# Seven half-size products for the up projections of the second FFN of a latent-diffusion backbone

## The chip, the cores and the metric

One Trainium2 chip; the program runs on one of its cores. Times are device microseconds of one execution, the median of the runs named beside them. The engines are TensorE (PE: matmuls; PEld: its weight loads), VectorE (DVE), ScalarE (ACT), GpSimd (POOL) and SyncE (SP, which issues most transfers). A granted TensorE clock of 1.00 is 2.4 GHz, one of 0.50 is 1.2 GHz.

## The reference

Two layers over 512 latent tokens and 256 context tokens of width 1024. Layer 0 mixes by attention, layer 1 by a bidirectional mLSTM; each is followed by a normalised, modulated, gated convolutional FFN with 2816 hidden channels. After layer 1 only the latent tokens are needed. What this document is about is the FFN of layer 1 and the normalisation ahead of it:

```python
x = x + gt2 * conv_ffn(modulate(rmsnorm(x, norm2_g[layer]), sh2, sc2),
                       ffn_w_up[layer], ffn_conv_w[layer], ffn_conv_b[layer], ffn_w_down[layer])

def conv_ffn(h, w_up, conv_w, conv_b, w_down):
    gate, val = jnp.split(jnp.dot(h, w_up), 2, axis=-1)
    return jnp.dot(jax.nn.silu(dwconv(gate, conv_w, conv_b)) * val, w_down)
```

`dwconv` is a convolution of width 3 over the tokens, channel by channel. Everything is float32.

## The kernel before

Activations lie with channels on the 128 partitions: `X` is [128, 8, 512], eight blocks of 128 channels by 512 tokens. To keep float32 accuracy a float32 product is made of three matmuls in the format float32r: both factors are cut into a high part (a cast, on ScalarE, L42) and a low part (the rest, a subtraction on VectorE, L43; together `split`), and high x high, low x high and high x low are added up in PSUM. `fm` (L77 to L86, its matmul is L85) does this for all blocks of the contraction.

Weights come in pieces of 512 KB. `weights` (L59) takes a raw tile `wr` of 128 x 1024, issues the load on SP (L66), and splits it into `wh` and `wl`. `wtile` (L48) hands these tiles out in turn: two buffers for `wr` at this point of the kernel, three each for `wh` and `wl`. A load waits until its raw buffer has been split, a split until the matmuls of its old contents are done.

PSUM has eight banks of 512 float32 columns: `A()` (L109) gives a pair of banks out of two pairs, `B(tags)` (L112) the banks T, U, R, O in turn, each one tile.

The hidden channels are 22 chunks of 128 (`NF`). `up(f)` (L319) makes one chunk: 24 matmuls of 512 columns for the gate, 24 for the value; the convolution (`conv`, L305 on ScalarE, L307 and L308 on VectorE), Silu (L339), the product with the value (L341), and the split of the result into `ah`, `al`. In chunks 0 to 3 of this layer `halves` cuts each matmul of 512 columns in two of 256, so that the first 256 tokens can be worked on while the second 256 are still being normalised. `down(fs)` (L359) takes a group of four chunks (the last group has two): for each of the eight output blocks 12 matmuls of 512 columns (L354) into one of the banks T, U, and an update of `X` on VectorE (`xupd`, L401). `ffn` runs up(0) to up(4), down of group 0, four more chunks, the next group, and so on; the last two groups come after all chunks. The last group's blocks are stored as soon as they are updated (L369).

Ahead of it (in `build`, at L1430) the last part of the layer's output projection runs in two halves of 256 tokens, six matmuls for each output block, and each half is followed by its norm: `norm_steps` (L256) sums squares (L269, L272 on ScalarE; L273 on VectorE and GpSimd), takes the reciprocal root, spreads it with a transpose into PSUM (L284), and then for each block of channels scales (`u`, L288, VectorE), adds the shift into the high part (L290, ScalarE), and forms the low part (L296 on VectorE for even blocks; L293 and L294 on ScalarE and GpSimd for odd ones).

The order of instructions on each engine is chosen by the framework when the program is built: it takes what it holds to be ready, by the order of the program text as priority. Each engine then runs its list strictly in order and waits where a semaphore says so. Tiles have their waits made by the framework.

Of the kernel before, what the change touches and what calls it, by code (L numbers as in the profile page):

```python
# [21 lines left out]
KD = 8  # L22
NF = 22
# [9 lines left out]
class Kernel:  # L33
    def __init__(self, tc, ins, out):
        self.tc, self.nc, self.i, self.out = tc, tc.nc, ins, out
        self.turn = {}


    def split(self, hi, lo, src, scale=None):
# [8 lines left out]
    def wtile(self, tag, n, cols, dt):  # L48

        bufs = [(self.wp, tag + "0"), (self.wp, tag + "1"), (self.wx, tag + "x")]  # L50
        if tag == "wr":
            del bufs[1]
        if self.wx is None:
# [202 lines left out]
    def norm_steps(self, pool, X, l, which, hh, hl, ranges):  # L256
# [4 lines left out]
        for t0, t1, c in ranges:  # L261
# [35 lines left out]

            steps += [lambda k=k, f=apply: f(k) for k in range(KD)]
        return steps


    def conv(self, y, ps, w, b, segs):
# [986 lines left out]
    def build(self):  # L1289
        tc, nc, i = self.tc, self.nc, self.i  # L1290
        with ExitStack() as es:
# [126 lines left out]
            gh = hp.tile([128, KD, NL], F32R, name="hh")  # L1418
            gl = hp.tile([128, KD, NL], F32R, name="hl")
            with tc.tile_pool(name="o1", bufs=1, reuse_waits="tile") as OP, \  # L1420
                    tc.tile_pool(name="nrm", bufs=1, reuse_waits="tile", side="right") as NP:
                x = [post(h, OP, "RO") for h in (6, 7)]
                for half in range(2):
                    t = slice(256 * half, 256 * half + 256)
                    for o in range(KD):
                        ps = self.B("TU")
                        m = 0
                        for (wh, wl), (xh, xl) in zip(ws, x):
                            for a, b in ((wh, xh), (wl, xh), (wh, xl)):
                                nc.tensor.matmul(ps[:, 0:256], a[:, o * 128:(o + 1) * 128], b[:, t],  # L1430
                                                 start=m == 0, stop=m == 5)
                                m += 1
                        self.xupd(1, 16, X, ps, o, 256 * half, 256, 0)
                    self.norm(NP, X, 1, 1, gh, gl, [(256 * half, 256 * half + 256, 0)])
            RP.release()


            with tc.tile_pool(name="ffn1", bufs=1, reuse_waits="tile") as FP:
                self.ffn(1, X, gh, gl, FP, NL, [])
            hp.release()  # L1440
            HP.release()

# [103 lines left out]
```

## Time and profile before

| what | value |
|---|---|
| median of 3 runs | 1748.17 us (1747.02 to 1748.54) |
| the profiled execution's own time | 1747.95 us |
| its span, first to last instruction | 1746.1 us |
| granted TensorE clock, mean | 0.989 |
| matmuls | 9622 |
| TensorE, VectorE, ScalarE, GpSimd busy | 96%, 72%, 43%, 15% of the span |
| moved by DMA | 169.43 MB, 97 GB/s on the mean |

Busy time of TensorE counts a matmul from its start to its modelled end, and matmuls overlap, so a busy TensorE is not one at its peak; how long a matmul takes in a stream is read from the distance of their starts, or from a block of the chain of waits divided by its count. The chain of waits follows the work that ended last backwards from the last instruction, at each step to what released it. "Idle" in a group of instructions is the time its engine stood still just before them.

### The profile page before, as it was taken

What the parts mean: (1) busy time and instruction counts of PE and PEld (TensorE: products, weight loads), DVE (VectorE), ACT (ScalarE), POOL (GpSimd) and SP (SyncE); (2) the same over time, 40 slices, a digit from 0 to 9 for tenths busy, and PEclk for the clock granted to TensorE, in tenths of its full rate; (3) what the DMA queues carried; (4) which work ended last, traced back from release to release, by engine and by line L of the source; (5) the groups of instructions that cost most, each with busy time, mean ns of one, the idle gap of its engine ahead of it and who ended that gap; (6) DMA issues with size and microseconds to landing.
All of it is one profiled execution on the core that took longest, in us unless ns stands there. A gap on an engine that the chain in (4) does not pass through costs nothing.

```text
span 1746.1 us, 25308 instructions
## 1 busy us (share of the span) xinstructions
PE 1673.7 (96%) x9622; PEld 1439.8 (82%) x9622; DVE 1250.8 (72%) x2310; ACT 749.6 (43%) x1394; POOL 261.3 (15%) x304
## 2 busy tenths in 40 slices
PE   6998898999999999999999989999999999999999
PEld 2787787888878888888888878888788898888887
DVE  7998889987787586675758467768778854444444
ACT  4336788986252132221312246645553542232231
POOL 0342545552120000000000023112110200000000
PEclk9999999999999999999999999999998999999999
DMA  8450000005344343342424233111112133323332
GB/s 315 127 167 24 11 11 13 14 1 207 107 140 150 97 146 120 124 154 88 154 85 134 72 121 98 61 50 37 61 43 103 61 109 97 97 97 97 98 97 96
DMA packets 73442, 169.43 MB, mean 97 GB/s; under 512 B 8292, under 2 KB 36964, under 8 KB 72936
## 3 DMA queue, kind: packets, MB, share of 16 engines
q1 hardware_dynamic: 73316, 167.80, 29.5%
q8 instruction: 76, 1.25, 0.3%
q14 instruction: 46, 0.38, 0.1%
q10 hardware_dynamic: 4, 0.01, 0.0%
HBM read 163.59 MB, written 4.20 MB: 96 GB/s over the span
## 4 chain that ended last, share of the span: by engine, by line
PE 73%; DVE 14%; ACT 7%; issue 3%; POOL 1%; DMA 1%; DVEq 0%; ACTq 0%; POOLq 0%; SPq 0%
PE psS L85 31%; PE psT L354 7%; PE psU L354 6%; PE psU L85 4%; PE psR L85 3%; PE psT L85 2%; DVE junk L138 2%; PE S L447 2%; PE psO L492 2%; PE psR L354 1%; PE psO L354 1%; ACT p L455 1%; PE state L1213 1%; DVE wl L43 1%; PE psT L95 1%
## 5 line engine op out<-in xcount | busy, mean ns | idle before, releaser
L85 PE MATMUL psS<-hl,wh 128*128 128x512 f32 (+1 forms) x992 | 346.8, 351 | 2.6 <-POOL hl L294 2.6
L85 PE MATMUL psS<-hh,wh 128*128 128x512 f32 (+1 forms) x992 | 347.0, 350 | 0.4 <-ACT hh L290 0.4
L85 PE MATMUL psS<-hh,wl 128*128 128x512 f32 (+1 forms) x992 | 346.1, 350 | 0.0
L42 ACT CAST wh<-wr 128x1024 fp32r<-128x1024 f32 (+2 forms) x187 | 193.4, 1036 | 338.6 <-PE psO L354 113.0
L43 DVE TENSOR_TENSOR wl<-wr,wh 128x1024 fp32r<-128x1024 f32 (+2 forms) x187 | 227.6, 1218 | 47.3 <-ACT wh L42 47.0
L85 PEld LDWEIGHTS psS<-hl,wh 128*128 128x128 f32 x992 | 186.8, 189 | 29.4 <-POOL hl L294 4.1
L85 PEld LDWEIGHTS psS<-hh,wh 128*128 128x128 f32 x992 | 186.8, 188 | 26.6 <-ACT hh L290 1.1
L85 PEld LDWEIGHTS psS<-hh,wl 128*128 128x128 f32 x992 | 186.6, 188 | 25.6
L307 DVE SCALAR_TENSOR_TENSOR y<-psS,fcw,y 128x511 f32<-128x511 f32 (+1 forms) x60 | 39.5, 658 | 143.3 <-ACT y L305 143.3
L138 DVE CUSTOM_DVE_ANT_0 y<-ar,cb 128x1024 f32<-128x1024 f32 x112 | 136.5, 1219 | 0.3 <-DMA ar<-in_ada 0.3
L305 ACT ACTIVATE y<-psS,fcb,fcw 128x512 f32<-128x512 f32 (+1 forms) x60 | 40.3, 705 | 205.3 <-PE psS L85 205.3
L273 POOL TENSOR_TENSOR sa<-sa,sq 128x256 f32<-128x256 f32 (+1 forms) x18 | 17.9, 993 | 637.1 <-ACT sq L272 637.1
L401 DVE SCALAR_TENSOR_TENSOR X<-psU,mod,X 128x512 f32<-128x512 f32 (+1 forms) x69 | 48.0, 696 | 87.3 <-PE psU L354 77.0
L458 POOL TENSOR_SCALAR p<-p,rs 128x768 f32<-128x768 f32 (+1 forms) x96 | 73.9, 776 | 114.7 <-DVE rs L457 70.5
L138 DVE CUSTOM_DVE_ANT_0 junk<-ar,cb 128x1024 f32<-128x1024 f32 x64 | 81.8, 1278 | 0.4
L341 DVE TENSOR_TENSOR y<-y,psS 128x512 f32<-128x512 f32 (+1 forms) x60 | 34.1, 597 | 52.8 <-PE psS L85 52.8
L354 PE MATMUL psT<-ah,wh 128*128 128x512 f32 x176 | 68.8, 391 | 1.8 <-DVE X L401 1.8
L339 ACT ACTIVATE y<-y 128x768 f32<-128x768 f32 (+1 forms) x44 | 32.6, 740 | 84.7 <-DVE y L308 84.7
L354 PE MATMUL psU<-ah,wh 128*128 128x512 f32 x176 | 68.7, 390 | 0.0
L354 PE MATMUL psU<-ah,wl 128*128 128x512 f32 x176 | 68.7, 390 | 0.0
L354 PE MATMUL psT<-ah,wl 128*128 128x512 f32 x176 | 68.7, 390 | 0.0
L354 PE MATMUL psU<-al,wh 128*128 128x512 f32 x176 | 68.5, 389 | 0.0
(674 smaller groups left out, 4382.9 us busy)
## 6 DMA issues: line engine op xcount, KB each, us to landing
ar<-in_ada SPq DMA_DIRECT2D x88, 512.0 KB, 3.5
wr<-in_wup SPq DMA_DIRECT2D x88, 512.0 KB, 3.4
wr<-in_wdn SPq DMA_DIRECT2D x44, 512.0 KB, 3.3
pr<-in_adak SPq DMA_DIRECT2D x8, 512.0 KB, 5.3
wr<-in_w_out SPq DMA_DIRECT2D x8, 512.0 KB, 3.5
wr<-in_w_mqk SPq DMA_DIRECT2D x8, 512.0 KB, 3.5
wr<-in_w_mv SPq DMA_DIRECT2D x8, 512.0 KB, 4.0
wr<-in_w_mo SPq DMA_DIRECT2D x8, 512.0 KB, 3.4
```

The costliest lines, as they stand in the source:

```text
L42: nc.scalar.copy(hi, src)
L43: nc.vector.tensor_tensor(lo, src, f32(hi), op=SUB)
L85: nc.tensor.matmul(ps, a, b[:, k, x0:x0 + n], start=i == 0, stop=i == 3 * nk - 1)
L138: nc.vector.tensor_tensor_reduce(out, raw, self.cb[:, c], 1.0, 0.0, MUL, ADD, self.mraw[l][:, n, c:c + 1])
L305: nc.scalar.activation(y[:, t0:t0 + n], p, AF.Identity, bias=b, scale=w[1])
L307: nc.vector.scalar_tensor_tensor(y[:, t0 + 1:t0 + n], p[:, 0:n - 1], w[0], y[:, t0 + 1:t0 + n], op0=MUL, op1=ADD)
L341: nc.vector.tensor_tensor(y[:, t0:t0 + n], y[:, t0:t0 + n], p, op=MUL)
L354: nc.tensor.matmul(ps[:, 0:n], x[:, off:off + 128], y[:, t0:t0 + n], start=m == 0, stop=m == 3 * len(fs) - 1)
L401: self.nc.vector.scalar_tensor_tensor(X[:, o, t0:t0 + n], ps[:, 0:n], self.mod[l][:, g0 + o, c:c + 1], X[:, o, t0:t0 + n], op0=MUL, op1=ADD)
L447: nc.tensor.matmul(s[:, c0:c0 + n], q[:, q0:q0 + 128], k[:, k0 + c0:k0 + c0 + n], start=m == 0, stop=m == len(passes) - 1)
L458: nc.gpsimd.tensor_scalar(p[:, 0:nk], p[:, 0:nk], r, 1.0, op0=MUL, op1=MUL)
L492: nc.tensor.matmul(out, a, b, start=st, stop=sp)
```

## The change

It replaces `norm` and `ffn` of layer 1 by `norm_seven` and `ffn_seven`; layer 0 keeps the old ones.

The up projection of a chunk is seen as a product of 2 x 2 blocks: the contraction in two halves of four channel blocks, the tokens in two halves of 256, and gate and value as the two rows. Seven products of half blocks (12 matmuls of 256 columns each) replace the eight (96 of 256, or 48 of 512). The sums of token halves that they need (T1 to T4) are made once, in `norm_seven`; the sums of weight blocks for each chunk: `R[:, 0]` and `R[:, 2]` are the value's second half and the gate's first half, each plus the value's first half, `R[:, 1]` is `R[:, 0]` plus the gate's first half. They are made by loading one summand three times over on SP and adding the others with two transfers that accumulate, issued by GpSimd; `R[:, 3]` adds the gate's second half to `R[:, 1]` on VectorE. Four pieces are split a chunk: the gate (A1), R0 and R1 (S12), R2 and R3 (S34), and the value's second half (`d`, half as long).

The products of a chunk share two accumulators: Y, one bank of a pair that two chunks share, and W, the second half of the bank whose first half is Z. Y is read after product 1, after 6, after 7 and after 4 while it goes on accumulating, W after product 5 and after 3. The loop is written out so that the products of chunk f stand between those of chunk f-1, with a step of the down projection (one output block, 12 matmuls of 512 columns) at two places of each turn. `wtile` gets one more buffer for each of the three tags.

```diff
+    def norm_seven(self, pool, X, l, B, half, n, kept):
...
+        for k in range(KD):
+            u = pool.tile([128, n], F32, tag="u", name="u", bufs=3)
+            nc.vector.scalar_tensor_tensor(u, X[:, k, t0:t1], s[:, k, 0:1], rb[:, 0:n], op0=MUL, op1=MUL)
+            sh = self.mod[l][:, 24 + k, 0:1]
+            nc.scalar.activation(h[:, k], u, AF.Identity, bias=sh)
+            if half == 0:
+                nm, kk = ("B11", k) if k < 4 else ("B21", k - 4)
+                nc.scalar.activation(B[nm][0][:, kk], u, AF.Identity, bias=sh)
+                low(nm, kk, h[:, k], nc.gpsimd if k % 2 else nc.vector)
+        if half == 0:
+            return
+        g = kept[0]
+        k2 = [(slice(a, a + 2), slice(a + 4, a + 6)) for a in (0, 2)]
+
+        for a, b in k2:
+            nc.vector.tensor_tensor(g[:, a], g[:, a], h[:, a], op=SUB)
+            nc.scalar.copy(B["T1"][0][:, a], g[:, a])
+            low("T1", a, g[:, a], nc.vector)
+        for a, b in k2:
+            nc.scalar.copy(B["B22"][0][:, a], h[:, b])
+            low("B22", a, h[:, b], nc.gpsimd)
+            nc.vector.tensor_tensor(h[:, a], h[:, b], h[:, a], op=SUB)
+            nc.vector.tensor_tensor(h[:, b], h[:, b], g[:, a], op=ADD)
+            nc.scalar.mul(B["T2"][0][:, a], h[:, b], -1.0)
+            nc.vector.scalar_tensor_tensor(B["T2"][1][:, a], h[:, b], -1.0, f32(B["T2"][0][:, a]), op0=MUL, op1=SUB)
+        for a, b in k2:
+            nc.scalar.copy(B["T3"][0][:, a], h[:, a])
+            low("T3", a, h[:, a], nc.gpsimd)
+        for a, b in k2:
+            nc.vector.tensor_tensor(g[:, b], h[:, b], g[:, b], op=SUB)
+            nc.scalar.copy(B["T4"][0][:, a], g[:, b])
+            low("T4", a, g[:, b], nc.vector)
+
+    def ffn_seven(self, l, X, B, pool):
...
+        def prod(ps, w, x, first, last):
+            m = 0
+            for k in range(4):
+                for a, b in ((w[0], x[0]), (w[1], x[0]), (w[0], x[1])):
+                    nc.tensor.matmul(ps, a[:, k], b[:, k], start=first and m == 0, stop=last and m == 11,
+                                     skip_group_check=True)
+                    m += 1
...
+        def load(f):
+            c = ch[f] = {}
+            g, v = i["wup"][l, f, 0], i["wup"][l, f, 1]
+            c["a"] = self.wtile("wr", KD, 128, F32)
+            nc.sync.dma_start(c["a"], g)
+            R = c["R"] = pool.tile([128, 4, 4, 128], F32, tag="R", name="R", bufs=2)
+            for j, src in enumerate((v[:, 4:8], v[:, 4:8], g[:, 0:4])):
+                nc.sync.dma_start(R[:, j], src)
+            c["d"] = pool.tile([128, 4, 128], F32, tag="d", name="d", bufs=2)
+            nc.sync.dma_start(c["d"], v[:, 4:8])
+            nc.gpsimd.dma_start(R[:, 0:3], v[:, 0:4].unsqueeze(1).to_broadcast([128, 3, 4, 128]), accum_op=ADD)
+            nc.gpsimd.dma_start(R[:, 1], g[:, 0:4], accum_op=ADD)
+
+        def p1(f):
...
+            c["A1"] = pair(c["a"])
+            prod(c["Y"], part(c["A1"], 0), B["B11"], True, False)
+
+        def p2(f):
+            c = ch[f]
+            zw = self.B("TU")
+            c["W"], Z = zw[:, n:2 * n], zw[:, 0:n]
+            prod(Z, part(c["A1"], 1), B["B21"], True, True)
+            g = c["g"] = pool.tile([128, nt], F32, tag="g", name="g", bufs=2)
+            nc.scalar.copy(g[:, 0:n], Z)
+            nc.vector.tensor_tensor(g[:, 0:n], g[:, 0:n], c["Y"], op=ADD)
+
+        def p5(f):
+            c = ch[f]
+            c["S12"] = pair(c["R"][:, 0:2].rearrange("p s k c -> p (s k) c"))
+            prod(c["W"], part(c["S12"], 0), B["T1"], True, False)
+            p = c["p5"] = pool.tile([128, n], F32, tag="p5", name="p5", bufs=2)
+            nc.scalar.copy(p, c["W"])
+
+        def p6(f):
+            c = ch[f]
+            prod(c["Y"], part(c["S12"], 1), B["T2"], False, False)
+            u = c["u2"] = pool.tile([128, n], F32, tag="u2", name="u2", bufs=2)
+            nc.scalar.copy(u, c["Y"])
+
+        def p3(f):
+            c = ch[f]
+            R = c["R"]
+            nc.vector.tensor_tensor(R[:, 3], R[:, 1], c["a"][:, 4:8], op=ADD)
+            c["S34"] = pair(R[:, 2:4].rearrange("p s k c -> p (s k) c"))
+            prod(c["W"], part(c["S34"], 1), B["B22"], False, True)
+            g = c["g"]
+            nc.vector.tensor_tensor(g[:, n:nt], c["u2"], c["W"], op=ADD)
...
+        def p7(f):
+            c = ch[f]
+            prod(c["Y"], part(c["S34"], 0), B["T3"], False, False)
+            v = c["v2"] = pool.tile([128, n], F32, tag="v2", name="v2", bufs=2)
+            nc.vector.tensor_tensor(v, c["p5"], c["Y"], op=ADD)
+
+        def p4(f):
+            c = ch[f]
+            prod(c["Y"], pair(c["d"], 4), B["T4"], False, True)
...
+        load(0)
+        for f in range(NF + 1):
+            for fs in groups:
+                if f == fs[-1] + 2:
+                    todo.append(down(fs))
+            if f + 1 < NF:
+                load(f + 1)
+            one, two = f < NF, f > 0
+            if one:
+                p1(f)
+            if two:
+                p7(f - 1)
+            go()
+            if one:
+                p2(f)
+                p5(f)
+                p6(f)
+            if two:
+                p4(f - 1)
+            go()
+            if one:
+                p3(f)
+        todo.append(down(groups[-1]))
+        while todo:
+            go()
```

In the first lines of `norm_seven`, left out above, squares are summed as in `norm_steps`. `low(name, k, src, engine)` subtracts a high part from its source on the engine named. `pair` splits a tile into `wh` and `wl` (for `d` into two tiles of its own). `go` issues one step of `down`; `down` is the old one, with banks R, O instead of T, U.

## Rows read from the trace of the kernel before

**Rows 1.** The page's head and its first part: busy time, share, instructions.

```profile
span 1746.1 us, 25308 instructions
PE 1673.7 (96%) x9622; PEld 1439.8 (82%) x9622; DVE 1250.8 (72%) x2310; ACT 749.6 (43%) x1394; POOL 261.3 (15%) x304
```

**Rows 2.** Chain of waits, 1300 us to the end: start, length, engine, tile, line, count.

```profile
1381.09 4.57 PE psS L85 x36
...
1403.77 11.52 PE psS L85 x96
...
1426.81 10.91 PE psS L85 x48
1437.71 2.72 PE psT L354 x12
...
1459.47 43.52 PE psS L85 x192
...
1655.32 54.40 PE psS L85 x240
...
1742.39 0.75 DVE X L401
```

**Rows 3.** Stretches: length, busy time of each engine, granted clock, DMA share, GB/s.

```profile
1299.00:1312.00 13.00, 10.22 (x55) 8.15 (x55) 11.28 (x29) 10.56 (x27) 2.52 (x2) 0.99 0.36 120
1312.00:1322.00 10.00, 9.40 (x40) 9.04 (x41) 8.06 (x18) 1.84 (x5) 0.00 (x0) 0.50 0.36 134
...
1362.00:1381.00 19.00, 15.03 (x110) 13.38 (x109) 16.09 (x44) 11.72 (x26) 6.54 (x8) 1.00 0.08 28
1381.00:1392.00 11.00, 10.75 (x85) 10.30 (x86) 9.89 (x27) 6.38 (x15) 3.91 (x6) 1.00 0.29 98
1500.00:1550.00 50.00, 50.00 (x223) 41.38 (x222) 24.68 (x28) 14.39 (x17) 0.00 (x0) 1.00 0.29 95
```

**Rows 4.** Timeline of VectorE, 1386 to 1400 us: start, length, instruction.

```profile
1386.42 1.26 DVE L288 SCALAR_TENSOR_TENSOR u<-X,s,psO 128x256 f32<-128x256 f32 x3 [0.59 <-PE psO L284]
...
1391.27 0.66 DVE L296 SCALAR_TENSOR_TENSOR hl<-u,mod,hh 128x256 fp32r<-128x256 f32 x1
```

**Rows 5.** Groups of instructions by form, 1360 to 1395 us.

```profile
L288 DVE SCALAR_TENSOR_TENSOR u<-X,s,psO 128x256 f32<-128x256 f32 x16 | 6.9, 474 | 0.8 <-PE psO L284 0.6
...
L401 DVE SCALAR_TENSOR_TENSOR X<-psU,mod,X 128x256 f32<-128x256 f32 x8 | 3.8, 481 | 1.5 <-PE psU L1430 1.4
...
L273 DVE TENSOR_TENSOR sa<-sa,sq 128x256 f32<-128x256 f32 x6 | 2.5, 416 | 0.0
```

**Rows 6.** Groups of instructions by form, 1420 to 1740 us.

```profile
L43 DVE TENSOR_TENSOR wl<-wr,wh 128x1024 fp32r<-128x1024 f32 x57 | 69.7, 1222 | 12.5 <-ACT wh L42 12.5
L42 ACT CAST wh<-wr 128x1024 fp32r<-128x1024 f32 x57 | 59.8, 1049 | 125.9 <-PE psU L354 80.7 <-PE psS L85 42.5 <-PE psR L85 2.7
...
L401 DVE SCALAR_TENSOR_TENSOR X<-psU,mod,X 128x512 f32<-128x512 f32 x23 | 17.3, 751 | 40.7 <-PE psU L354 40.7
...
L307 DVE SCALAR_TENSOR_TENSOR y<-psS,fcw,y 128x511 f32<-128x511 f32 x18 | 13.5, 750 | 62.6 <-ACT y L305 62.6
L43 DVE TENSOR_TENSOR al<-y,ah 128x512 fp32r<-128x512 f32 x19 | 13.0, 685 | 0.0
L341 DVE TENSOR_TENSOR y<-y,psS 128x512 f32<-128x512 f32 x18 | 12.4, 688 | 36.8 <-PE psS L85 36.8
```

**Rows 7.** Waits of TensorE, 1355 to 1395 us: total, times, longest.

```profile
PE psS L85 <- POOL hl L294: 1.6, 2, 1.4
...
PE psU L1430 <- DVE X L401: 0.6, 1, 0.6
```

**Rows 8.** Transfers by issue, whole span: count, KB each, median us to landing.

```profile
wr<-in_wup SPq DMA_DIRECT2D x88, 512.0 KB, 3.4
...
X<-in_xT SPq DMA_DIRECT2D x4, 768.0 KB, 8.4
...
out<-X SPq DMA_DIRECT2D x8, 256.0 KB, 2.0
```

More of the change, by code (lines that the diff above doesn't have):

```diff
@@ L299, in norm_steps, with low @@
         return steps
+    def norm_seven(self, pool, X, l, B, half, n, kept):
+        nc = self.nc
+        t0, t1 = half * n, half * n + n
+        if half == 0:
+            self.s = self.gains(l, 1)
+        s = self.s
+        sa = [pool.tile([128, n], F32, tag=f"sa{e}", name="sa", bufs=1) for e in range(2)]
+        for k in range(KD):
+            if k < 2:
+                nc.scalar.square(sa[k], X[:, k, t0:t1])
+            else:
+                sq = pool.tile([128, n], F32, tag="sq", name="sq", bufs=2)
+                nc.scalar.square(sq, X[:, k, t0:t1])
+                (nc.vector if k % 2 else nc.gpsimd).tensor_tensor(sa[k % 2], sa[k % 2], sq, op=ADD)
+        nt = n // 128
+        pv = self.B("R")
+        for j in range(nt):
+            for e in range(2):
+                nc.tensor.matmul(pv[:, j:j + 1], sa[e][:, j * 128:(j + 1) * 128], self.oD, start=e == 0, stop=e == 1)
+        v = self.sm.tile([128, nt], F32, tag="nv", name="nv")
+        nc.vector.tensor_scalar(v, pv[:, 0:nt], EPS, None, op0=ADD)
+        r = self.rsqrt(v, nt, "n")
+        rb = self.B("O")
+        for j in range(nt):
+            nc.tensor.transpose(rb[:, j * 128:(j + 1) * 128], r[:, j:j + 1].to_broadcast([128, 128]), self.ident)
+        h = kept[half] = pool.tile([128, KD, n], F32, tag=f"h{half}", name="h", bufs=1)
+        def low(name, k, src, eng):
+            eng.tensor_tensor(B[name][1][:, k], src, f32(B[name][0][:, k]), op=SUB)
+        for k in range(KD):
+            u = pool.tile([128, n], F32, tag="u", name="u", bufs=3)
[6 more added lines that the diff above has]
+                low(nm, kk, h[:, k], nc.gpsimd if k % 2 else nc.vector)
+        if half == 0:
+            return
[19 more added lines that the diff above has]
+            low("T4", a, g[:, b], nc.vector)
@@ L1417, in build @@
             hp = tc.alloc_tile_pool(name="h3", bufs=1, reuse_waits="tile")
-            gh = hp.tile([128, KD, NL], F32R, name="hh")
-            gl = hp.tile([128, KD, NL], F32R, name="hl")
+            B = {nm: [hp.tile([128, 4, NL // 2], F32R, tag=nm + e, name=nm + e) for e in "hl"]
+                 for nm in ("B11", "B21", "B22", "T4")}
+            z = HP.tile([128, KD, T], F32R, tag="hl", name="Ts").rearrange("p k t -> p (k t)").rearrange(
+                "p (j k t) -> p j k t", j=6, k=4)
+            B.update({nm: [z[:, 2 * j], z[:, 2 * j + 1]] for j, nm in enumerate(("T1", "T2", "T3"))})
+            kept = {}
             with tc.tile_pool(name="o1", bufs=1, reuse_waits="tile") as OP, \
@@ L1433, in build @@
                         self.xupd(1, 16, X, ps, o, 256 * half, 256, 0)
[L1434 removed]
+                    self.norm_seven(NP, X, 1, B, half, 256, kept)
             RP.release()
             with tc.tile_pool(name="ffn1", bufs=1, reuse_waits="tile") as FP:
[L1439 removed]
+                self.we = FP
+                self.ffn_seven(1, X, B, FP)
+                self.we = None
             hp.release()
```

61 lines of the change are left out of this document (added).

## The prediction

> **What bounds the kernel now.** I read first the page's head and engine table: TensorE is busy 96% of a span of 1746.1 us [rows 1]. Because that share says little about one stage, I read next the chain of waits over the last 400 us. From about 1381 us to 1742.4 us it is nothing but matmuls of the second FFN, one block after another, then one VectorE update of 0.75 us [rows 2]. The table by stretches says the same: in 1500 to 1550 us TensorE has 50.00 of 50 us, VectorE 24.68, ScalarE 14.39, and the DMA engines a share of 0.29 [rows 3]. So here every matmul taken out is time taken out, as long as nothing else becomes late.
>
> The chain also prices a matmul. 96 of 256 columns take 11.52 us, 0.120 us each; 192 of 512 columns take 43.52 us, 0.2267 us each [rows 2]. Half the columns cost 53% of the time, not 50%: some 13 ns of each are fixed (2 x 0.120 less 0.2267). The change cuts columns but raises the number of matmuls, so this matters.
>
> **The products.** Before, a chunk of 128 hidden channels takes 48 matmuls of 512 columns; chunks 0 to 3 take 96 of 256 instead. Up projections in all: 4 x 11.52 + 10.91 (chunk 4) + 17 x 10.88 = 241.9 us [rows 2]. After, each chunk is 7 products of 12 matmuls of 256 columns: 84 x 0.120 = 10.08 us, times 22 = 221.8 us. **Term 1: -20.2 us**, not the eighth (30 us) that the multiplication count promises. The down projection keeps its blocks of 2.72 us [rows 2]; a chunk with its share of it takes 10.08 + 5.44 = 15.52 us instead of 16.32.
>
> **The start.** Products 1 and 2 need only the first 256 tokens, the others sums over both halves. In the old kernel VectorE runs the second half's norm from 1386.42 to 1391.93 us [rows 4]; meanwhile TensorE works on first-half columns and is busy 10.75 of 11.00 us from 1381 us on [rows 3]. In the new norm VectorE has after 1386.42 us: 8 scalings x 0.474 [rows 5], T1 with 4 operations of 512 columns x 0.685, the loop of T2 with 2 x (0.685 + 0.685 + 0.75), T4 with 4 x 0.685 [rows 6]: 13.5 us. Chunks 0 and 1 want between these three splits of 1.222, one weight sum and one half split of 0.685 [rows 6]: 5.0 us more, so all is there at 1404.9 us. Until then TensorE can run products 1, 2, 5, 3, 6 of two chunks, 10 x 1.44 = 14.4 us, from 1381.1 us: 9.4 us idle where there was 0.25. Some splits can run ahead, so I take 8 us. Low end 3 us (the splits and half of T4 hidden). High end: the same 9.4 us and a clock at half. After a broken stretch at 1299 to 1312 us (10.22 of 13 us busy) the granted clock was 0.50, the level of 1.2 GHz, for the next 10 us, but the gaps of 1362 to 1381 us (15.03 of 19 us busy) left it at 1.00 [rows 3]; half speed for 10 us costs 5 us, so 14.4 us. **Term 2: +8 us (3 to 14.4).**
>
> The Trainium skill (TensorE: Matmul & The Clock Gate, HAM oscillation) says that waits between bursts of matmuls throttle the clock again and the next burst begins slow. By it the high end would hold and the sum below would be 6.4 us higher; the trace has one stretch for it and one against.
>
> **Chunks 1 to 4** run before any down projection can fill in. VectorE's work a chunk: splits 3 x 1.222 + 0.685, weight sum 0.685, convolution 2 x 0.75, last split 0.685 [rows 6], three sums out of PSUM x 0.48 and two products x 0.42 [rows 5]: 9.5 us against TensorE's 10.08. That is 94%, so one waits for the other here and there: **Term 3: +1 us (0 to 3).** From chunk 5 on the down projection adds 1.222 + 2 x 0.751 [rows 6], 12.2 of 15.52 us: hidden. ScalarE has 4 full splits x 1.049 [rows 6] and about as much in small copies and activations, some 8.3 us: hidden too, whatever cover goes.
>
> **Handoffs.** The old loop gave each product a bank and a whole chunk to be read. Now product 5 writes the bank from which ScalarE copies Z, and 6, 7 and 4 pile onto Y after reads by VectorE and ScalarE. In program order other products or a block of 2.72 us lie between, except from 2 to 5. What is queued behind a waiting matmul is all of TensorE. Low end 0 (below nothing is excluded: TensorE has no idle time to win back there [rows 3]). High end: one unfilled handoff a chunk. The nearest wait of this kind is TensorE for VectorE's update of X, 0.6 us [rows 7]; a copy of 0.48 [rows 5] with a release on either side comes to 0.75. I take 0.25 a chunk, since most have filler: **Term 4: +5.5 us (0 to 16.5).**
>
> The Trainium skill (PSUM — Partial Sum Buffer, PSUM bank collisions raise a hardware error) has readers and the writer of a bank kept apart by bank, not by address, so W cannot be written while Z is read. By it the high end would hold unless the order fills it, and the sum would be 11 us higher; the old kernel never shares a bank so, and no row shows it.
>
> **The weight sums.** A chunk's loads go from two to five on SP, and two accumulating transfers on GpSimd: 768 KB that waits for three of the loads, then 256 KB that waits for the first. GpSimd is otherwise idle by then (0 in 1500 to 1550 us [rows 3]); nothing stands behind them but the next pair. No accumulating transfer is in the trace. As plain transfers they would be between 3.4 us (512 KB) and 8.4 us (768 KB in a busy queue), and 2.0 us (256 KB) [rows 8]; I take 4.1 + 2.0 = 6.1 us, nearer the first because DMA has a share of only 0.29 here. What depends on them: the fourth weight sum, then the release of the chunk's raw tile, into which the down projection's next weights load. The loop closes over two chunks: split S34 2.3, loads 5.5 (estimated from 3.4 for one and about 0.7 for each of three more), sums 6.1, weight sum 0.7, down weights 3.4, their split 2.3: 20.3 us against 2 x 15.52 = 31.0. Covered, with 10.7 us to spare: **Term 5: 0**; if the cover goes, see the second rival.
>
> **The end.** Last block, 0.75 us update and store are unchanged: 0.
>
> **Sum:** -20.2 + 8 + 1 + 5.5 = -5.7 us on the profiled execution's 1747.95 us, 1742.2; the median is 0.2 us above that execution, so 1742.4. All low ends together (-17.2) give 1731, all high ends (+13.7) 1762.
>
> **Rivals.** (a) *Handoffs are not filled*: one wait of 0.75 us a chunk: 1742.4 + 11 = 1753.4, slower. For it: the shared bank and VectorE at 79%, in pieces of 1.2 us. Against it: the old trace packs short dependent groups with waits of at most 0.6 us [rows 7]. It decides from 0.5 us a chunk on. (b) *The sums come late*: a queue of accumulating transfers takes the place of TensorE. If they take m times 6.1 us, the loop is 14.2 + 6.1 m and passes 31.0 at m = 2.75. At m = 3.5 it is 35.6, 17.8 us a chunk, 2.3 us over, times 17 chunks with a down share: 1742.4 + 39 = 1781, slower. For it: an accumulation reads the target as well as the source, which may double it; nothing measured excludes more. Against it: 10.7 us of slack. (c) *The start eats the gain*, the half clock included: 1742.4 + 6.4 = 1748.8, no change; for it, the broken stretches at 1299 and 1362 us [rows 3]; against it, that ready splits can run ahead. (d) *The start is hidden and the handoffs filled*: -17.2, 1731.
>
> **How the numbers follow.** Forecast 0.42, (d) 0.18, (c) 0.10, (a) 0.13, (b) 0.17. A measurement tells 0.2%, 3.5 us, from no change: bounds 1744.7 and 1751.7. The likeliest case's own range is 1735 to 1750, of its 0.42 some 0.30 below the first bound. Faster: that and (d), 0.48. Within: 0.10 of the forecast and (c), 0.20. Slower: the rest of it, (a) and (b), 0.32. The range goes from 1730 to 1768: it leaves out the late part of (b), some 0.12, and 0.05 below.
>
> **What would show it.** Right: groups of 12 matmuls of 256 columns 1.44 us apart; a hole of some 8 us between 1381 and 1405 us; TensorE busy over 98% after that; accumulating transfers landing within 6 to 12 us a pair. (a) would show as waits of TensorE for ScalarE's copy of Z or VectorE's sums, (b) as waits of the splits for R or of the raw tile. The forecast is wrong if TensorE's idle time after chunk 5 is over 12 us in all, or if a matmul of 256 columns in the new order takes more than 0.125 us.

## The result and the profile after

The kernel with the change takes 1864.8 us (median of 4 runs, 1860.1 to 1872.5) against 1747.6 of the kernel before: ratio 1.068, 95% interval 1.063 to 1.072. It is 117 us slower, and far outside the range given. The profiled execution has a span of 1870.6 us.

Lines of the page (its head, busy times, transfers by issue: count, KB each, median us to landing), answering to [rows 1] and, for the new transfers, [rows 8]:

```profile
span 1870.6 us, 27080 instructions
PE 1698.6 (91%) x10222; PEld 1483.5 (79%) x10222; DVE 1332.0 (71%) x2475; ACT 811.5 (43%) x1514; POOL 314.0 (17%) x348
...
R<-in_wup POOLq DMA_DIRECT2D x22, 768.0 KB, 7.3
...
R<-in_wup POOLq DMA_DIRECT2D x22, 256.0 KB, 4.5
```

No engine has become the bound: TensorE lost share and no other came near it. The new thing is a pair of accumulating transfers a chunk that take 7.3 + 4.5 = 11.8 us. The table by stretches (columns as in [rows 3]) says where time went:

```profile
1380.00:1400.00 20.00, 4.34 (x30) 4.12 (x28) 17.82 (x34) 11.14 (x25) 12.08 (x8) 0.67 0.08 20
1400.00:1420.00 20.00, 7.44 (x48) 7.15 (x49) 7.47 (x11) 5.57 (x8) 1.75 (x2) 0.60 0.89 200
...
1500.00:1550.00 50.00, 43.24 (x276) 39.24 (x274) 24.82 (x36) 18.03 (x26) 5.25 (x5) 0.93 0.64 161
```

Two losses, then. At the start TensorE is busy 11.8 of 40 us, at a granted clock of 0.6 to 0.7. And in the steady part, where it had 50.00 of 50 us [rows 3], it has 43 (40 to 45 in the other stretches up to 1850 us), at a clock of 0.93 (0.87 to 0.93). The waits of TensorE (for what; total us, times, longest) name the first as one wait of 27.8 us for the cast of the first weight sums (S12 of chunk 0), and split the second over many waits for sums out of PSUM:

```profile
PE Y L390 <- DVE v L467: 33.3, 9, 5.3
PE psT L390 <- ACT wh L43: 27.8, 1, 27.8
PE psU L390 <- ACT g L432: 18.8, 8, 3.2
```

Those sums and copies are short (0.4 us), so the list of waits does not say why they are late. The chain of waits does. From one fourth weight sum (`R[:, 3]`, L451) to the next, in the steady part (start, length, what):

```profile
1592.38 0.69 DVE R L451
1593.08 0.66 DVE y L458
...
1593.99 0.74 DVE y L459
1594.73 1.05 DVE wl L44
...
1595.78 0.43 DVE y L474
...
1596.27 0.43 SPq L411
...
1596.74 3.38 DMA R<-in_wup
...
1600.79 6.80 DMA R<-in_wup
1607.59 4.86 issue
1612.44 0.69 DVE R L451
```

TensorE is not in it. It is a ring: VectorE's queue 3.8 us, the plain loads into R 3.9, the first accumulation 7.5, the second 4.85 (issued at 1607.88; the chain prints it as "issue"): 20.06 us, **one chunk for each turn of the ring**, where a chunk's matmuls need 15.7. The timeline of VectorE (start, length, instruction, idle time before it) at the next turn shows what ties it:

```profile
1606.40 0.41 DVE L455 TENSOR_TENSOR g<-u,psT 128x256 f32<-128x256 f32 x1
1612.44 0.69 DVE L451 TENSOR_TENSOR R<-R,wr 128x512 f32<-128x512 f32 x1 [5.63 <-issue]
1613.05 0.74 DVE L458 SCALAR_TENSOR_TENSOR y<-g,fcw,y 128x511 f32<-128x511 f32 x1
...
1614.50 0.41 DVE L467 TENSOR_TENSOR v<-p,Y 128x256 f32<-128x256 f32 x1
1614.83 1.22 DVE L44 TENSOR_TENSOR wl<-R,wh 128x1024 fp32r<-128x1024 f32 x1
```

VectorE stands 5.63 us for L451, the fourth weight sum of chunk f+1, whose accumulation has not landed. Behind it in its list is the low part `wl<-R` of S34 of chunk **f**; ScalarE made the high part at 1608.41. That low part is the last reader of chunk f's buffer of R, and the loads of chunk f+2 wait for that buffer. It ends at 1616.05 (1614.83 and 1.22 more), and SP issues the loads at once:

```profile
1616.07 1.28 SPq L411 DMA_DIRECT2D R<-in_wup  x3
```

(The chain names `y` L474 ahead of the loads, but that runs from 1615.96 to 1616.38, and SP does not wait for it.) R has two buffers, but with this order one can be refilled only after the other has been summed: the loads of two chunks are never under way together.

The start, on GpSimd's timeline:

```profile
1388.01 4.57 POOL L333 TENSOR_TENSOR B22l<-h,B22h 128x512 fp32r<-128x512 f32 x2 [5.46 <-ACT B22h L354]
...
1395.54 1.60 POOL L333 TENSOR_TENSOR Ts<-h,Ts 128x512 fp32r<-128x512 f32 x1 [1.28 <-ACT Ts L361]
1397.08 2.80 POOL L414 DMA_DIRECT2D R<-in_wup  x2
```

The plain loads of chunks 0 and 1 had been issued from 1372.71 us on, but the accumulations stand in GpSimd's list behind its share of the new norm, and are issued at 1397.08.

### The profile page after: what moved, and what is told of

Same layout as the page of the kernel before. It is cut to its first block, busy times and chain, and to the rows that moved or that the text cites. A ratio compares the mean times of both kernels' runs of the same rounds, so it can differ in the third digit from the quotient of the medians.

```text
span 1870.6 us, 27080 instructions
## 1 busy us (share of the span) xinstructions
PE 1698.6 (91%) x10222; PEld 1483.5 (79%) x10222; DVE 1332.0 (71%) x2475; ACT 811.5 (43%) x1514; POOL 314.0 (17%) x348
## 4 chain that ended last, share of the span: by engine, by line
PE 53%; DVE 17%; DMA 13%; issue 9%; ACT 7%; POOL 2%; SPq 0%; POOLq 0%; DVEq 0%; ACTq 0%
PE psS L88 18%; DMA R<-in_wup 12%; PE psU L88 4%; PE psT L588 3%; PE psU L588 3%; DVE wl L44 2%; PE psR L88 2%; PE psT L88 2%; DVE junk L141 2%; PE S L681 1%; PE psO L588 1%; PE psR L588 1%; PE psO L726 1%; PE psO L493 1%; PE psR L98 1%
## 5 line engine op out<-in xcount | busy, mean ns | idle before, releaser
L88 PE MATMUL psS<-hl,wh 128*128 128x512 f32 (+1 forms) x640 | 216.6, 339 | 1.1 <-POOL hl L297 1.1
L88 PE MATMUL psS<-hh,wh 128*128 128x512 f32 (+1 forms) x640 | 216.5, 339 | 0.4 <-ACT hh L293 0.4
L88 PE MATMUL psS<-hh,wl 128*128 128x512 f32 (+1 forms) x640 | 216.0, 338 | 0.0
L88 PEld LDWEIGHTS psS<-hl,wh 128*128 128x128 f32 x640 | 120.5, 188 | 16.4 <-POOL hl L297 2.1
L88 PEld LDWEIGHTS psS<-hh,wh 128*128 128x128 f32 x640 | 120.4, 188 | 15.1 <-ACT hh L293 0.9
L88 PEld LDWEIGHTS psS<-hh,wl 128*128 128x128 f32 x640 | 120.2, 188 | 14.4
L276 POOL TENSOR_TENSOR sa<-sa,sq 128x512 f32<-128x512 f32 (+1 forms) x12 | 13.5, 1124 | 590.2 <-ACT sq L275 590.2
L451 DVE TENSOR_TENSOR R<-R,wr 128x512 f32<-128x512 f32 x22 | 15.2, 691 | 126.9 <-issue 104.5
L390 PE MATMUL Y<-Ts,wh 128*128 128x256 f32 x352 | 82.7, 316 | 8.4 <-DVE y L473 7.1
L44 DVE TENSOR_TENSOR wl<-R,wh 128x1024 fp32r<-128x1024 f32 x44 | 53.7, 1221 | 33.0 <-ACT wh L43 32.9
L390 PEld LDWEIGHTS Y<-Ts,wh 128*128 128x128 f32 x352 | 68.6, 226 | 9.7 <-DVE y L473 7.3
L684 DVE TENSOR_REDUCE nm<-S 128x1 f32<-128x768 f32 x64 | 60.1, 945 | 2.0 <-PE S L681 1.6
```

What stands on the lines that cost most here:

```text
L44: nc.vector.tensor_tensor(lo, src, f32(hi), op=SUB)
L88: nc.tensor.matmul(ps, a, b[:, k, x0:x0 + n], start=i == 0, stop=i == 3 * nk - 1)
L390: nc.tensor.matmul(ps, a[:, k], b[:, k], start=first and m == 0, stop=last and m == 11, skip_group_check=True)
L684: nc.vector.tensor_reduce(nm, s[:, 0:nk], axis=AX.X, op=MAX, negate=True)
```

## The experiments

Theory A: the steady loss is the ring over one chunk, closed by VectorE's order. Its rival: the accumulations are too long, or too many for the queues, whatever the order. Theory B: the start's loss is the accumulations' place in GpSimd's list; its rival: the sums of tokens and casts are late anyway. (In the expectations, written before this text, theory B is the rival of A, and what is called theory B here is theory C there.) Runs without an interval are single ones, each beside a run of the kernel before (1746.2 us).

**1. The order alone.** The low part of S34 must be issued ahead of the next fourth sum (`self.s34` is that low part of the chunk before).

```diff
-            nc.vector.tensor_tensor(R[:, 3], R[:, 1], c["a"][:, 4:8], op=ADD)
+            if f:
+                with self.tc.issue_after(self.s34.ins):
+                    nc.vector.tensor_tensor(R[:, 3], R[:, 1], c["a"][:, 4:8], op=ADD)
...
```

> The changed kernel with one edge more: on VectorE the weight sum R[:,3] of chunk f+1 is issued behind the last split (S34, low part) of chunk f, where it had stood ahead of it. Nothing else is changed: the same buffers, transfers and matmuls. Theory A (VectorE's order closes the loop of the transfers over one chunk, 20.4 us): the loop now spans two chunks, TensorE sets the pace from chunk 5 on at 15.6 to 17 us a chunk, and the time falls by 16 x 4 to 16 x 4.8 us, from 1865 to about 1790 to 1805 us. Theory B (the transfers themselves, 1 MB accumulated a chunk, take 20 us whatever the order): no change, 1850 to 1875 us. The idle stretch of some 28 us at the start stays in both.

Measured 1792.65 us, in the range of theory A: 72 us less than with the change, from one exchanged pair on one queue. The fourth sums (L453 in this kernel) and the low parts (of S12 at 1590.10, of S34 at 1597.65), on VectorE's timeline:

```profile
1585.28 0.69 DVE L453 TENSOR_TENSOR R<-R,wr 128x512 f32<-128x512 f32 x1 [2.68 <-issue]
1590.10 1.23 DVE L44 TENSOR_TENSOR wl<-R,wh 128x1024 fp32r<-128x1024 f32 x1 [2.00 <-ACT wh L43]
...
1597.65 1.22 DVE L44 TENSOR_TENSOR wl<-R,wh 128x1024 fp32r<-128x1024 f32 x1
...
1601.85 0.69 DVE L453 TENSOR_TENSOR R<-R,wr 128x512 f32<-128x512 f32 x1 [2.64 <-issue]
```

A chunk now takes 16.5 us (115.3 us between the sums at 1502.69 and 1618.01, seven chunks) instead of 20.7 (103.5 for five). Each sum still waits 2 to 3 us and holds what is behind it, so it is not quite 15.7. Theory A is shown; the transfers are the same ones as before.

**2. A third buffer for R**, which breaks the ring without touching an order.

```diff
-            R = c["R"] = pool.tile([128, 4, 4, 128], F32, tag="R", name="R", bufs=2)
+            R = c["R"] = pool.tile([128, 4, 4, 128], F32, tag="R", name="R", bufs=3)
```

> The changed kernel with three buffers for R instead of two. VectorE's order keeps the next chunk's weight sum ahead of this chunk's last split, but the loads of chunk f+2 now go to a buffer that was freed a chunk earlier. Theory A: two chunks' transfers in flight, the pace is TensorE's, 15.6 to 17 us a chunk, about 1785 to 1805 us. Theory B (throughput of the accumulating transfers): 1850 to 1875 us, with the same 20 us a chunk.

Measured 1780.51, a little under theory A's range. In its stretches the steady loss is gone altogether, with accumulations of 7.6 and 4.7 us and DMA engines 84% busy. What is left is the start, with chunks 1 to 4, whose sums come late too (1440 to 1460 us):

```profile
1380.00:1400.00 20.00, 6.10 (x34) 5.88 (x33) 17.05 (x35) 10.78 (x23) 10.43 (x8) 0.59 0.21 79
1400.00:1420.00 20.00, 5.11 (x24) 4.61 (x24) 7.02 (x12) 5.22 (x10) 5.58 (x6) 0.53 1.01 203
1420.00:1440.00 20.00, 19.68 (x157) 18.89 (x157) 14.57 (x22) 11.33 (x16) 3.45 (x3) 1.00 0.95 233
1440.00:1460.00 20.00, 10.12 (x61) 9.68 (x61) 8.69 (x13) 6.64 (x11) 4.31 (x4) 0.82 0.89 205
...
1500.00:1550.00 50.00, 50.00 (x347) 45.90 (x346) 35.09 (x50) 24.44 (x36) 6.99 (x7) 1.00 0.84 210
```

**3. The accumulations left out** (of the computation this leaves out the added terms of `R[:, 0]` to `R[:, 2]`, and with them part of `R[:, 3]`).

```diff
-            nc.gpsimd.dma_start(R[:, 0:3], v[:, 0:4].unsqueeze(1).to_broadcast([128, 3, 4, 128]), accum_op=ADD)
-            nc.gpsimd.dma_start(R[:, 1], g[:, 0:4], accum_op=ADD)
```

> The changed kernel without its two accumulating transfers a chunk: the weight blocks are used unsummed (this leaves out the weight sums, all else is kept). It measures what the rest of the change is worth. Theory A and B alike: the loop of 20.4 us loses the 12 us of both transfers and TensorE sets the pace; by the prediction's other terms (start 3 to 14, chunks 1 to 4 0 to 3, handoffs 0 to 16.5 us) 1731 to 1762 us, 1742 by the sum. If it stays over 1762 us the handoffs or the start were priced too low as well.

Measured 1753.08: inside the range expected, but still 6.9 us above the kernel before, although the seven products themselves save. That it lies in the range is luck: the handoffs cost less than the sum had for them and the start more (see the next section). Steady, a pair of chunks takes 31.34 us (fourth sums at 1527.23 and 1558.57), so 15.67 a chunk against 16.32 before [rows 2], with TensorE at 50.00 of 50. The start is not free without accumulations either: one wait of 16.9 us until 1403.03. ScalarE's list shows where it ends; the cast of chunk 0's sums stands behind the casts of T4 and two copies, though its plain loads had long landed:

```profile
1400.74 0.62 ACT L365 CAST T4h<-h 128x512 fp32r<-128x512 f32 x1 [0.57 <-DVE h L364]
1401.39 0.37 ACT L430 COPY g<-psT 128x256 f32<-128x256 f32 x1
1401.66 0.38 ACT L430 COPY g<-psU 128x256 f32<-128x256 f32 x1
1401.92 1.06 ACT L43 CAST wh<-R 128x1024 fp32r<-128x1024 f32 x1
```

A kernel with another order on ScalarE was not tried, so that this order costs the 16.9 us is read, not shown. VectorE's low part of the same sums comes no earlier (1403.01, behind the last low part of T4), so another order on ScalarE alone would not give all of it back.

**4 and 5. The norm's low parts on VectorE**, so that GpSimd's list holds nothing ahead of the accumulations; alone, and with the third buffer of R.

```diff
-            low("B22", a, h[:, b], nc.gpsimd)
+            low("B22", a, h[:, b], nc.vector)
...
-            low("T3", a, h[:, a], nc.gpsimd)
+            low("T3", a, h[:, a], nc.vector)
```

(The odd blocks of B11 and B21 likewise.)

> The changed kernel with the low parts of the norm (B11 and B21 of odd blocks, B22, T3) subtracted on VectorE instead of GpSimd, so that nothing stands ahead of the first accumulating transfers in GpSimd's queue. Theory C (the first sums wait in GpSimd's order behind these subtractions, from 1378 to 1397 us): the idle stretch of TensorE at the start, 28 us, falls to 10 to 16 us, and the time by 10 to 16 us, to about 1850 us. Rival (the token sums T1 to T4 on VectorE set the start): no change or up to 8 us slower, since VectorE has some 8 us more to do.

> Three buffers for R and the low parts of the norm on VectorE together. With the loop over one chunk gone the start should show in the time. Theory C (the first sums wait in GpSimd's order): the idle stretch at the start falls from 28 to about 15 us and the time from 1780.5 to 1764 to 1770 us. Rival (a shorter stretch at the start is given back in chunks 1 to 4, where the transfers are late anyway): 1776 to 1782 us.

Alone: the wait at the start falls from 27.8 to 14.8 us, as expected, but the 10 to 16 us less in time do not show: 1860.92 lies among the change's own four runs (1860.1 to 1872.5). With the ring in force the earlier start is, it seems, mostly given back. With three buffers: 1763.39, 17.1 us below run 2 and just under the range expected. GpSimd's timeline of that run:

```profile
1377.48 1.48 POOL L414 DMA_DIRECT2D R<-in_wup  x1 [3.76 <-DVE u L337]
1380.75 1.28 POOL L414 DMA_DIRECT2D R<-in_wup  x1 [1.79 <-DMA R<-in_wup]
1387.54 0.89 POOL L415 DMA_DIRECT2D R<-in_wup  x1 [5.51 <-DMA R<-in_wup]
```

So moving the low parts off GpSimd is worth 17 us of the start; 14.7 us of wait for the cast stay, much as in run 3. Theory B is shown for most of the 17 us, but not for all (run 3, with no accumulation at all, still waits 16.9 us of run 2's 28.2): the edit does a second thing. While GpSimd subtracts, three of VectorE's own instructions on the token sums take 1.74 to 1.75 us each, where without it they take 0.68. The same line with the change, then in run 5:

```profile
1391.40 1.74 DVE L357 TENSOR_TENSOR h<-h 128x512 f32<-128x512 f32 x1 [1.16 <-POOL B22l L333]
1391.56 0.68 DVE L357 TENSOR_TENSOR h<-h 128x512 f32<-128x512 f32 x1
```

**6. Plain transfers on GpSimd's queue in place of accumulating ones** (of the computation this leaves out the additions: the second source overwrites the first).

```diff
-            nc.gpsimd.dma_start(R[:, 1], g[:, 0:4], accum_op=ADD)
+            nc.gpsimd.dma_start(R[:, 1], g[:, 0:4])
```

(The 768 KB transfer likewise.)

> The changed kernel with its two GpSimd transfers a chunk as plain copies, without the addition (this leaves out the weight sums; sizes, queue and waits are kept). It prices the accumulation itself. Theory A: the chunk's loop is the sum of its parts, so it shortens by what the transfers shorten: from 7.3 and 4.5 us to landing to about 4.5 and 2.5 us, 20.4 to about 15.6 us a chunk, and the time to 1775 to 1800 us. Rival (the 2 us or so of GpSimd's issue and the fixed part of a transfer are the cost, not the addition): landing stays at 6 us and more, over 19 us a chunk, 1845 us or more.

Measured 1806.7, between the two: the transfers got shorter by less than expected. By issue:

```profile
R<-in_wup POOLq DMA_DIRECT2D x22, 768.0 KB, 5.3
R<-in_wup POOLq DMA_DIRECT2D x22, 256.0 KB, 3.3
```

8.6 us instead of 11.8: 3.2 us off the ring, and the ring's turn goes from 20.7 to 17.8 us (107.0 between the sums at 1504.78 and 1611.74, six chunks). That is still over 15.7, so TensorE still waits. So adding costs these transfers 37% over writing, not double.

**7. The sums by GpSimd additions**, without accumulating transfers; the value weights come in one tile of their own, and `g`, `p5`, `u2` and `v2` have one buffer each to make room.

```diff
-            nc.gpsimd.dma_start(R[:, 0:3], v[:, 0:4].unsqueeze(1).to_broadcast([128, 3, 4, 128]), accum_op=ADD)
-            nc.gpsimd.dma_start(R[:, 1], g[:, 0:4], accum_op=ADD)
+            b = pool.tile([128, KD, 128], F32, tag="b", name="b", bufs=2)
+            nc.sync.dma_start(b, v)
+            c["d"], ga = b[:, 4:8], c["a"][:, 0:4]
+            nc.gpsimd.tensor_tensor(R[:, 0], b[:, 4:8], b[:, 0:4], op=ADD)
+            nc.gpsimd.tensor_tensor(R[:, 1], R[:, 0], ga, op=ADD)
+            nc.gpsimd.tensor_tensor(R[:, 2], b[:, 0:4], ga, op=ADD)
```

> The weight sums R0, R1, R2 by three additions on GpSimd from one whole load of the value's weights, instead of three loads and two accumulating transfers; R with two buffers, VectorE's order as the planner makes it. Theory A: load 3.5 us and three additions of 1.5 to 2.2 us take the place of 3.4 + 7.3 + 4.5 us in the loop over one chunk, which falls to about 13 us, so that TensorE sets the pace (15.7 us a chunk as without the sums). The start keeps GpSimd's subtractions ahead of the first sums: an idle stretch of 20 to 24 us. 1754 to 1764 us. Rival (GpSimd and VectorE slow each other down on additions with two inputs from SBUF): over 17 us a chunk, 1780 us or more.

Measured 1793.39: my expectation failed. The additions take 4.9 us a chunk (1.53, 1.61 and 1.74 us in the groups of 1500 to 1700 us), but a chunk takes 16.9 us, not 15.7: R and the new tile have two buffers each, and GpSimd waits 96.0 us for that tile's loads in these 200 us. The rival is in the trace too: beside GpSimd's additions VectorE's instructions are longer than in run 2 (L459 1.58 us on the mean against 0.75, the low parts from R 1.50 against 1.22), VectorE waits 12.7 us for the sums, and TensorE 10.9 us for VectorE's `g`, about 1 us a chunk. The run changes the slimmed buffers too, so how its loss divides stays open.

**8 to 11. Versions meant to beat the kernel before.** Run 2 leaves the start, so here chunks 0 to 2 are made by eight products, which need no weight sum, while the sums of chunk 3 are fetched. R has three buffers; `g`, `p5`, `u2`, `v2`, `d` one each.

```diff
+            if f < 3:
+                c["b"] = self.wtile("wr", KD, 128, F32)
+                nc.sync.dma_start(c["b"], v)
+                return
...
-            one, two = f < NF, f > 0
+            if f < 3:
+                eight(f)
+                continue
+            one, two = f < NF, f > 3
```

> Three buffers for R, and chunks 0 to 2 by the eight products of the old kernel (96 matmuls of 256 columns, no sums of tokens or weights needed), so that the token sums, the subtractions on GpSimd and the first weight sums run beside 3 x 11.5 us of matmuls; five small tiles have one buffer instead of two to make room. If the start (28 us idle, half clock, chunks 1 to 4 short of sums) is the whole rest of the loss of the run with three buffers, 1780.5 us, the time falls below that of the kernel before: 1735 to 1743 us. If chunks 3 to 6 still wait for their sums, 1745 to 1760 us.

Measured 1767.41, above both ranges. TensorE's early wait only moved: 14.1 us between 1420 and 1440 us. SP's waits show the reason in one row, the plain loads of chunk 3 held until 1399.57 us by a tile of the norm in whose memory R lay:

```profile
SPq L415 <- DVE Ts L359: 19.3, 1, 19.3
```

Runs 9 and 10 lay R out first, ahead of everything else in that pool, and issue its loads and accumulations for three chunks behind the loads of chunk 1; run 10 also moves B22's and T3's low parts to VectorE.

```diff
+        Rs = {f: pool.tile([128, 4, 4, 128], F32, tag="R", name="R", bufs=3) for f in range(3, 6)}
...
+            if f == 0:
+                for e in Rs:
+                    loadr(e)
```

> As the run with eight products for chunks 0 to 2, and the plain transfers into R and their accumulations for chunks 3, 4 and 5 are taken out of the chunks' own loads: the three R buffers are the first thing laid out in the FFN's memory, where nothing of the norm lies, and their transfers stand on the queues behind the loads of chunk 1 and ahead of those of chunk 2. Nothing of the arithmetic changes. Theory (at the start TensorE waits for sums whose plain transfers were released too late, because R lay over the norm's tiles, until 1399.6 us): the accumulations go out at about 1397, behind GpSimd's last subtraction, and the first sums are done at about 1410, before chunk 3 asks for them; the 18.6 us of idle TensorE between 1420 and 1460 go, and some 5 us of half clock with them: 1767.4 - 23.6 = 1744, between 1740 and 1750. Rival (the start is short of transfer bandwidth, not of an early release: 12 plain and 6 accumulating transfers beside the down weights keep the DMA engines over 90% busy): the wait only moves, at least 10 us of idle remain between 1400 and 1460, 1754 to 1768.

> The run before it, with the low parts of B22 and T3 subtracted by VectorE and not by GpSimd, so that the accumulations stand behind B12's low parts, at about 1388 us, and not behind the last of T3 at 1397. Theory (GpSimd's order sets when the accumulations begin, but with eight products for three chunks there is room until about 1415): the same time within 3 us, 1741 to 1749; the first weight sum of VectorE is ready some 9 us earlier and nothing waits for it. Rival (bandwidth): the earlier start takes 5 to 9 us off whatever idle time between 1400 and 1460 the run beside it shows. It loses 1 to 3 us if VectorE, 17.8 of 20 us busy between 1380 and 1400, then makes the inputs of TensorE late.

Run 9: 1757.3 us, ratio to the kernel before 1.0046 (1.0031 to 1.0062); run 10: 1766.6, 1.0100 (1.0083 to 1.0117). Both theories failed: 1740 to 1750 and 1741 to 1749 were expected. Run 9 lies in its rival's range, with 8.0 us of idle TensorE left between 1400 and 1460 where the rival had at least 10 and the theory none. The early loads won some 10 us, but neither run beats the kernel before. Run 10 changed more than its edit: SP's list now has R's nine plain loads behind a weight load of chunk 2, so they go out at 1399.73 us instead of 1381.85, and the first accumulation at 1406.80 instead of 1398.65. The framework had re-ordered the lists around the moved subtractions. In run 9 TensorE's largest wait is much the old pattern: a sum that waits for a transfer, and behind it what another engine needs. VectorE's timeline (L482 is the fourth sum here):

```profile
1444.64 0.69 DVE L482 TENSOR_TENSOR R<-R,wr 128x512 f32<-128x512 f32 x1 [7.37 <-issue]
1445.25 0.75 DVE L489 SCALAR_TENSOR_TENSOR y<-g,fcw,y 128x511 f32<-128x511 f32 x1
1445.91 0.41 DVE L498 TENSOR_TENSOR v<-p,Y 128x256 f32<-128x256 f32 x1
```

A sum that waits for its transfer holds the convolution and the v that TensorE needs for 6.5 us. Run 11 puts the sum behind that v, writes B22 in the norm's own loop, and lets the eight products go by halves of the tokens (against run 9):

```diff
-            nc.vector.tensor_tensor(R[:, 3], R[:, 1], c["a"][:, 4:8], op=ADD)
+            with self.tc.issue_after(vl.ins) if vl is not None else ExitStack():
+                nc.vector.tensor_tensor(R[:, 3], R[:, 1], c["a"][:, 4:8], op=ADD)
...
-                nm, kk = ("B12" if half else "B11", k) if k < 4 else ("B21", k - 4)
+                nm, kk = (("B11", "B21"), ("B12", "B22"))[half][k // 4], k % 4
```

> As the run with eight products for chunks 0 to 2 and early transfers (ratio 1.0046), with two more edits. VectorE's sum of chunk f may be issued only after the v addition of chunk f-1, so that a sum still waiting for its accumulations holds up nothing that TensorE needs; and B22 is written in the norm's own loop, right after B12, while the eight products of a chunk go by halves of the tokens (both matrices on half 0, then both on half 1), so that TensorE has work while half 1 is normed. Theory (what is left of the start's loss is one wait of 6.5 us, TensorE behind VectorE's v addition behind a sum of the next chunk, and 29.5 of 40 us of busy TensorE, half of it at half clock, between 1360 and 1400, where the kernel before has 35.8 at full clock): the wait goes, and 5 to 10 us of the stretch 1360 to 1400 come back: 11 to 16 us less, ratio 0.9955 to 0.999. Rival (transfer bandwidth between 1400 and 1440, where the DMA engines are 81 to 101% busy, sets when chunk 5's sum is done, whatever the order): the wait of 6.5 us stays as a wait on another instruction, only the start's part is won, ratio 0.999 to 1.003.

1758.0 us, ratio 1.0064 (1.0051 to 1.0077): no gain, and above the ranges of theory and rival. The wait of 6.5 us is gone as meant, and two others came, as the waits of TensorE from 1350 us on say:

```profile
PE psR L389 <- DVE wl L44: 5.9, 1, 5.9
PE psO L525 <- ACT wh L43: 2.7, 1, 2.7
```

The first is chunk 1's low part of a weight, behind the norm's token sums on VectorE, which is busy 18.94 of 20 us between 1380 and 1400. The balance of run 11 nearly closes. Chunks 0 to 2 take 96 matmuls of 256 columns in both kernels; the other 19 save 15.8 us in products (chunk 3 1.44, the rest some 0.80 each). The down projection loses 3.5 (next section). TensorE is idle 16.8 us in 1360 to 1500 us where the kernel before has 4.2 (+12.6), and 1.7 us more between 1550 and 1720. The stretches at clocks of 0.83 to 0.96 cost some 6.3 us, an estimate (busy time times the missing part of the clock). Together +8.3; the span is 8.7 us longer. None of the versions tried beats the kernel before.

## Why the prediction was wrong

Taken apart by the runs, the 117 us are: products -20.2; down projection +3.5; start +23.5 without accumulations (run 3: 6.9 above before, plus the 16.7 that products and down projection save); +27.4 more at the start through the accumulations (run 2 less run 3); +84 through the ring (the change less run 2). Each of the last three is a difference that rests on single runs, and the 84 could be 80 to 92, by the change's own four runs. The two of the start agree with the stretches of 1360 to 1500 us: TensorE is idle there 4.2 us in the kernel before, 22.2 in run 3 and 43.9 in run 2, and what the lower clock takes comes on top.

**Term 5, the weight sums, is the step that failed**, at the words "The loop closes over two chunks". The accumulations take 11.8 us, 1.93 times the 6.1 assumed and under the 2.75 at which the prediction saw trouble; by its pieces a loop over two chunks would be 14.2 + 11.8 = 26.0 us against 31. But two buffers give a loop over two chunks only if the consumer of buffer f comes ahead of the producer's next step on every queue that both use. The prediction asked what is queued behind a waiting matmul on TensorE; of VectorE, where the change adds a wait for a transfer (L451), it did not ask what stands behind it. Behind it stood the release of the other buffer.

The pieces were not complete either. Run 1 has the loop over two chunks, and its turn is 32.7 us, from the sum at 1585.28 by the low part of S34 at 1597.65 to the sum at 1618.01. 12.4 us of that lie between a fourth sum and the low part of S34, where the prediction had only a sum and a split (0.7 + 2.3): ScalarE's high part waits for TensorE until 1596.52. So run 1 stays 12 us above run 2, and only with the third buffer does nothing wait in the steady part. (The text of the change has one more buffer for each of `wtile`'s three tags; in the code `wh` and `wl` get one, and `wr`, the raw tile of this loop, keeps two.)

**Rival (b)** had the place ("the sums come late", waits for R) and the sign, with 0.17. Its mechanism, transfers 2.75 times as long, is not what happened, and its price of 39 us, for transfers 3.5 times as long, still came from a loop of two chunks; the loop of one cost 84.

**Term 2, the start** (+8, from 3 to 14.4): 51 us by runs 2 and 3. Two steps failed. "Until then TensorE can run products 1, 2, 5, 3, 6 of two chunks": 5 needs weight sums, and with the accumulations issued at 1397 these came at 1411 to 1412 us; the line "GpSimd is otherwise idle by then" rested on a row from 1500 us [rows 3] and was used for the start too, where GpSimd's own low parts were in front (17 us by runs 2 and 5, with what VectorE gains there). And some ready splits did not run ahead (run 3). A price was off as well: VectorE's 13.5 us of norm and token sums took 16.2 (1384.01 to 1400.26), with three instructions at 1.74 to 1.75 instead of 0.685 and 1.16 us of waiting for GpSimd. The clock made it worse: after the long wait the stretch 1400 to 1420 has 0.60; in run 2 it has 0.53, then 1.00, and 0.82 again in the stretch with the next waits. That is what the rule cited from the Trainium skill (TensorE: Matmul & The Clock Gate, HAM oscillation) says of a burst after a wait, and the prediction's high end of 5 us for it was near the right size (4.4 us in 1380 to 1420, in run 2 4.9, an estimate from busy time and clock), but only as an addition to a gap three times as long.

**Term 1** was right. A product's 12 matmuls are 1.44 us apart, 0.120 each. What it missed is the down projection: its 12 matmuls of 512 columns take 2.80 us here, 0.2333 each, where they took 2.72 [rows 2]; 22 chunks x 24 x 0.0067 = 3.5 us in all. "Keeps its blocks of 2.72 us" is where it went wrong.

**Term 3** (+1) was about right for what it priced: in run 3, where no sum is waited for, TensorE has 19.48, 20.00 and 20.00 of 20 us from 1420 to 1480. With the accumulations the sums of these chunks come late: run 2 has 19.68 of 20 us in 1420 to 1440, but 10.12 in 1440 to 1460. That is counted with the start.

**Term 4, the handoffs** (+5.5, rival (a) +16.5 in all): nothing. A chunk's 15.67 us in run 3 are its products and two blocks of the down projection, 10.08 + 5.60. TensorE's timeline in run 3, between the last matmul of Z and the first of product 5 into the same bank:

```profile
1566.84 0.28 PE L390 MATMUL psT<-B21l,wh 128*128 128x256 f32 x1
1566.95 0.28 PE L390 MATMUL Y<-T4h,dh 128*128 128x256 f32 x1
...
1567.31 0.28 PE L390 MATMUL Y<-T4h,dh 128*128 128x256 f32 x1
1567.58 0.39 PE L390 MATMUL psT<-Ts,wh 128*128 128x256 f32 x1
```

ScalarE copies Z from 1567.15 for 0.37 us, and product 5 begins at 1567.58, right after. The gap is filled with the first matmuls of the other chunk's product 4: product 4 is cut in two there. The bank rule (PSUM — Partial Sum Buffer, PSUM bank collisions raise a hardware error, of the Trainium skill) is kept here by order and costs nothing, so the end that it would have set did not hold.

The sign that the text named for a wrong forecast, over 12 us of idle TensorE after chunk 5, is what the trace shows: 5 to 10 us in every 50 from 1500 to 1850 us.

## What to carry to other kernels

Before counting a double buffer as cover, write down for each engine that touches both buffers what stands behind an instruction that waits for a transfer; if the release of the other buffer is there, the loop is one step long, not two. An order made at build time by priorities can do this without any dependency asking for it, and a third buffer or one forced pair of instructions takes it away (84 and 72 us of the 117 here). And a queue that is idle in the steady part may be the busiest one at the start: look at the cover of a new transfer at the place of its first use.

## What was not expected of the hardware

- The accumulating transfers took 7.3 us for 768 KB and 4.5 us for 256 KB; plain ones of the same shape on the same queue 5.3 and 3.3 (run 6). Issuing one held GpSimd 1.28 and 0.90 us, a plain one 0.75 and 0.56.
- A matmul of 512 columns comes every 0.2333 us in the stage with the products of 256 columns, in the kernels with the seven products, and every 0.2267 in the kernel before, both at a granted clock of 1.00. The products beside it are not the cause: in run 2 no product runs after 1749.6 us, and the last 108 matmuls are still 0.232 us apart on the mean. No run looked further; it stays open.
- An addition of 512 columns took GpSimd 1.53 to 1.74 us (run 7) where VectorE's of the same size takes 0.69. And while GpSimd computes, some of VectorE's instructions take more than twice their time (1.74 against 0.68 us, runs 4 and 5 above).
